# Moving the gating of w_down into the up-projection's stage, and one level of the recurrence's copies to ScalarE

## The chip, the core and the metric

The kernel runs on one core of one Trainium2 chip. The metric is the device time of one launch in microseconds; before the change it is 2444.8 us (median of three runs, 2444.23 to 2445.5). Five engines work in parallel, each in its own order: TensorE (PE) multiplies matrices, VectorE (DVE), ScalarE (ACT) and GpSimd (POOL) work elementwise, and SyncE (SP) issues nearly all DMA transfers. An instruction that has to wait holds up everything behind it on its engine; on SP that is every later transfer.

## The reference

One layer of a hybrid backbone on 2048 latent tokens of width 1024 (and 256 context tokens), in float32:

```
h  = modulate(rmsnorm(x), sh1, sc1)
o  = token_mixers(h @ w_in)        # HGRN2 recurrence (4 heads) and gMLP spatial gating (4 heads)
x  = x + g1 * (o @ w_out)
h2 = modulate(rmsnorm(x), sh2, sc2)
x  = x + g2 * ((a * gelu(conv3x3(g))) @ w_down)     # a, g = split(h2 @ w_up), 2816 columns each
out = rmsnorm(x)
```

The gates g1 and g2 are vectors over the 1024 output columns, computed from c and w_ada. Since g2 multiplies every row of the last product alike, the kernel multiplies the columns of w_down by g2 once and stores the result ("gating of w_down"). The recurrence is evaluated in chunks of 128 positions by doubling: within a chunk the scores between positions are filled in by levels of 1, 2, 4, ... 64, where a level B holds the pairs in neighbouring blocks of B positions.

## The kernel before, in words

The kernel runs in four stages after a short start (first 100 us: modulation vectors and the context).

1. Input projection and recurrence, to about 980 us. `run_banks` walks over column blocks of w_in: 24 matmuls of 128x512 per bank, in three terms (high and low parts of both operands, float32r). Between them `slot()` asks two queues whether the next piece of other work is due: `hg_q` holds the recurrence of the previous head (`hg`), `bg_q` the background work. Due times are kept in `T.t`, a clock that adds up the expected time of every issued matmul; a generator yields how many us of it must pass before its next piece. In order, the background holds eight blocks of the modulation (`ada_block`), the gating and splitting of w_out (`w_out_ops`), the convolution's taps (`conv_taps`), and the gating of w_down (`w_down_ops`).
2. Output projection and second norm, to about 1169 us. Its results, prepared as seven operands of a Strassen-like product, partly stay in SBUF and partly go through DRAM (`yd`); the staging tiles have the tag `yst`, two buffers.
3. Up-projection and convolution, to about 2014 us: 308 products of 12 matmuls each, two units (a `g` unit and an `a` unit, two column blocks of w_up each) interleaved in groups of 14. Each product's weights are loaded as `raw` halves (512 KB), split by `prep` three products ahead (`LOOK = 3`): ScalarE casts the high part `Ah`, GpSimd subtracts to get the low part `Al`, four buffers each. The 12 matmuls take the high part first, eight times, then the low part four times. `after` empties the PSUM banks (`ux`, `uz`, two each): copies `keep` on ScalarE, additions on VectorE. The convolution is nine taps over a 128x1024 tile: one on ScalarE (L1431), eight on VectorE (L1434, in place in PSUM tile `dn`), then GELU on ScalarE. Results go to DRAM as `m`, edge rows through `gs` and `as`.
4. Down-projection, to the end: seven products of 11 column pairs, operands `m` and the gated w_down (`wd_d`, eleven DRAM tiles) read back and split. It reads the gated w_down first shortly before the third stage ends.

`T.t` decides where work is written into the program. After that a planner orders the instructions of each engine by its own expected times; `pin(...)` keeps an instruction in the order in which it was written. Neither knows the time that the chip takes.

The gating of w_down (L997 to L1011) takes two halves of the columns: g2 broadcast to 128 partitions (L1004), and for each of 11 row pairs a load of 512 KB into a `raw` tile (L1007; three buffers, shared with the loads of w_in, L221), a pinned VectorE multiplication of 128x1024 (L1009) and a store (L1010).

In a recurrence level, TensorE forms the products of a level for eight chunks in two banks of tag `sc`. Levels up to 32 are merged into the score tile `sc` with a predicated VectorE copy by a mask (L846, 128x512), the level of 64 by two ScalarE copies of 64 partitions x 4 x 64 (L843, L844). After each level VectorE scales Q (`level_update`, L513), K is scaled and copied (`level_keys`, VectorE or GpSimd L590, ScalarE L593), and the totals are multiplied (`next_tot`, L520).

Of the kernel before, what the change touches and what calls it, by code (L numbers as in the profile page):

```python
# [9 lines left out]
F32 = mybir.dt.float32  # L10
F32R = mybir.dt.float32r
# [7 lines left out]
P = 128  # L19
# [9 lines left out]
NF = FF // P  # L29
# [4 lines left out]
AL = 512  # L34
# [14 lines left out]
def view(t, off, dims):  # L49

    return bass.AP(t.tensor, t.offset + off, [list(t.ap[0])] + [list(d) for d in dims])
# [32 lines left out]
def tile_trunk(ctx, tc, x, c, cx, c_ctx, w_ada, b_ada, norm_mix, norm_ffn, w_in, hg_norm, sgu_g, sgu_b,  # L84
               w_sp, b_sp, w_out, w_up, conv_w, conv_b, w_down, norm_final, masks, out):
    nc = tc.nc
    V, S, G, T = nc.vector, nc.scalar, nc.gpsimd, Tensor(nc.tensor)
    ld = nc.sync.dma_start
    st = nc.sync.dma_start
    pin = tc.keep_in_program_order  # L90

    x = x[0]
    w_ada, w_in, w_out, w_up, w_down = w_ada[0], w_in[0], w_out[0], w_up[0], w_down[0]
# [21 lines left out]
    g_d = dr.tile([2, D], F32, name="g_d")  # L115
# [4 lines left out]
    wd_d = [dr.tile([P, 2, D], F32, name=f"wd{j}") for j in range(NF // 2)]  # L120
# [62 lines left out]
    hg_q, bg_q = Pump(), Pump()  # L183
# [7 lines left out]
    with es1:  # L191
        ps = es1.enter_context(tc.tile_pool(name="ps1", bufs=1, space=PSUM, reuse_waits="tile"))
        p1 = es1.enter_context(tc.tile_pool(name="p1", bufs=1, reuse_waits="tile"))
        pm = es1.enter_context(tc.tile_pool(name="pm", bufs=1, reuse_waits="tile"))
# [19 lines left out]
        def raw_tile():  # L214
            return p1.tile([P, D], F32, tag="raw", name="raw", bufs=3)
# [51 lines left out]
        acc = ph.tile([P, 2, 512], F32, tag="qs", name="acc")  # L267
# [523 lines left out]
        def hg(hh, h, F, K, qs, vt, sgt):  # L791
# [33 lines left out]
            for l, B in enumerate(LV):  # L825
                dims = [[2 * B, P // (2 * B)], [TH + B, 2], [1, B]]
                if B < 4:
                    dims = [[TH + B, 2], [2 * B, P // (2 * B)], [1, B]]
                if B == P // 2:
                    dims = dims[1:]  # L830
                for g in range(0, NCH, 4):
                    pb = bank("sc")
                    if B == 1:
                        column_sums(pb, knh[g // 4], knl[:, g * P:g * P + 512])
                    for i in range(4) if B > 1 else ():
                        off = (g + i) * P
                        o = pb[:, i * P:(i + 1) * P]
                        if B < 4:
                            o = view(pb, i * P, [[B, 2], [2 * B, P // (2 * B)], [1, B]])
                        T.matmul(o, K[:, 0, off:off + P], view(Q, off, dims), start=True, stop=True)  # L840
                    if B == P // 2:
                        pq = pb.rearrange("p (c t) -> p c t", t=P)
                        S.copy(sc[:B, g:g + 4, B:], pq[:B, :, B:])  # L843
                        S.copy(sc[B:, g:g + 4, :B], pq[B:, :, :B])  # L844
                        continue
                    V.copy_predicated(sc[:, g:g + 4, :], view(msk, l * P, [[0, 4], [1, P]]),  # L846
                                      pb.rearrange("p (c t) -> p c t", t=P))
                level_update(Q, TH, B, tot, False)
                K, K2 = level_keys(K, B, tot, K2), None
                tot = next_tot(tot, TH, B)  # L850
                yield 4.2
# [144 lines left out]
                    st(wo_d[:, k, 1, cl], g)  # L996
                    yield 2.5  # L997

        def w_down_ops():

            for n in range(2):
                cl = slice(n * 512, n * 512 + 512)
                g = pm.tile([P, 512], F32, tag="acc", name="g2")
                ld(g, g_d[1:2, cl].broadcast_to([P, 512]))  # L1004
                for j in range(NF // 2):
                    raw = raw_tile().rearrange("p (a c) -> p a c", a=2)
                    ld(raw, w_down[2 * j * P:2 * (j + 1) * P, cl].rearrange("(a p) c -> p a c", p=P))  # L1007
                    yield 9.0
                    pin(V.tensor_mul(raw, raw, view(g, 0, [[0, 2], [1, 512]])))  # L1009
                    st(wd_d[j][:, :, cl], raw)  # L1010
                    yield 2.5  # L1011

        def silu(dst, scale):
            def f(n0, n, pj):
                t = pm.tile([P, 512], F32, tag="sig", name="sig", bufs=2)
# [4 lines left out]
        def head(hh, h):  # L1020
# [18 lines left out]
            def pre_g():  # L1039
                if prev[0] >= 0:  # L1040
                    need(hg_q, (prev[0], prev[1], "keys"))
                else:
                    need(bg_q, "x1")
                    for e in range(8):
                        bg_q.add(ada_block(e))
                    bg_q.add(w_out_ops())
                    bg_q.add(conv_taps())
                    bg_q.add(w_down_ops())
                t["F"] = pk.tile([P, 2, TH], F32, tag="F", name="F", align_bytes=AL)
                t["K"] = pk.tile([P, 2, TH], F32, tag="K", name="K", bufs=2, align_bytes=AL)  # L1050

# [479 lines left out]

    NJ = NF // 2

    def a_src(r, c, j):
        return m_d[2 * j + c][:, r * TH:(r + 1) * TH]

# [30 lines left out]
    for n, (u, i) in enumerate(prods):  # L1567
# [20 lines left out]
        if n == 12:  # L1588
            edges = px.tile([P, 7, P], F32R, tag="yst", name="edges", bufs=2, align_bytes=AL).bitcast(F32)
            edges = edges[:, :4, :].rearrange("p f (w c) -> p f w c", w=2)  # L1590
        with tc.issue_after(scaled[-1].ins) if n < 8 else nullcontext():
            after(u, i, p)
        for j in range(7):
# [13 lines left out]
            cast(j, early[j], wr[j], (mhl[:, j, 0, :], mhl[:, j, 1, :]),  # L1607
                 [t.rearrange("p a b -> p (a b)") for t in a_tiles()])
        conv_step() and conv_step()
    assert not work  # L1610
    while stores:
        stores.pop(0)[1]()
    esp.close()
# [250 lines left out]
```

## Time and profile before

| what | us |
|---|---|
| median of three runs | 2444.8 |
| profiled execution | 2441.35 |
| its span, first to last instruction | 2439.6 |
| TensorE busy | 2403.6 (99%) |
| VectorE busy | 1669.5 (68%) |
| ScalarE busy | 1039.4 (43%) |
| GpSimd busy | 882.7 (36%) |

The profile is one execution; times in its rows are us from the span's start, and durations marked "mean" or min/median/max are ns. The page gives busy time by engine; other views group instructions by line and tile, give busy time by stretches, list who waited for whom (in total, times, longest), and show a stretch in order of time. In the timeline a row is: start, length, engine, line, operation, output tile and inputs, form, count, and in brackets the idle time before it and what ended it. "SPq" is SP's queue of transfers; its rows show when a transfer is issued, not when it lands. Consecutive rows of a kind are merged, and matmuls overlap, so a matmul shows 0.39 us while the next starts 0.227 us after it. Line numbers are those of the kernel before.

### The profile page before, as it was taken

The numbers are of one execution on the slowest core, as the hardware profiler recorded it, in microseconds if no ns is written. First come the engines' busy times: TensorE is split into PE (matmuls) and PEld (weight loads), VectorE is DVE, ScalarE is ACT, GpSimd is POOL, SyncE is SP. The second block draws the span as 40 slices with busy tenths as digits, with TensorE's granted clock in tenths as the row PEclk, the third lists the DMA queues.
The fourth block names the chain that finished last, engine by engine and source line by source line (L and its number), as shares of the span: only waits on it lengthen the run. The fifth ranks groups of instructions, "written<-read, shape, count | busy, mean of one in ns | idle before, by whom it ended". The sixth has DMA issues, their size and how long they took to land.

```text
span 2439.6 us, 32382 instructions
## 1 busy us (share of the span) xinstructions
PE 2403.6 (99%) x11711; PEld 1995.0 (82%) x11711; DVE 1669.5 (68%) x2293; ACT 1039.4 (43%) x1802; POOL 882.7 (36%) x796
## 2 busy tenths in 40 slices
PE   8999999999999999999999999999999999999998
PEld 5887887888888887788888888888888887888887
DVE  5867795756776786465596666639866772776875
ACT  4554334434444443354554444434445442332343
POOL 1232110110121132000688778787888870000002
PEclk9999999999999999999999999999999999999999
DMA  8365446573354323768922322562222238934745
GB/s 311 108 209 163 152 136 196 193 241 121 113 177 156 104 104 141 239 209 260 309 82 86 97 81 91 183 230 97 86 94 86 88 112 334 324 121 147 229 153 196
DMA packets 307853, 400.10 MB, mean 164 GB/s; under 512 B 33113, under 2 KB 216161, under 8 KB 304621
## 3 DMA queue, kind: packets, MB, share of 16 engines
q1 hardware_dynamic: 304404, 397.28, 48.3%
q8 instruction: 92, 1.51, 0.2%
q10 hardware_dynamic: 3289, 0.76, 0.1%
q14 instruction: 68, 0.56, 0.1%
HBM read 288.85 MB, written 109.13 MB: 163 GB/s over the span
## 4 chain that ended last, share of the span: by engine, by line
PE 47%; issue 2%; POOL 1%; DVE 1%; ACT 1%; SPq 0%; DMA 0%; POOLq 0%; ACTq 0%
PE ux L65 19%; PE uz L65 14%; PE dn L65 14%; POOL ra L1723 0%; POOL rr L1724 0%; DVE dn L1434 0%; POOL Al L134 0%; ACT mhl L133 0%; ACT jk L1715 0%; DVE odd L80 0%; ACT odd L1793 0%; DVE mhl L80 0%; DVE thl L80 0%; ACT thl L133 0%; POOL raw L1243 0%
## 5 line engine op out<-in xcount | busy, mean ns | idle before, releaser
L1434 DVE SCALAR_TENSOR_TENSOR dn<-gp,taps,dn 128x1024 f32<-128x1024 f32 x352 | 448.3, 1285 | 97.2 <-ACT dn L1431 92.8
L65 PE MATMUL dn<-thl,mhl 128*128 128x512 f32 x1680 | 381.5, 389 | 1.2 <-ACT thl L133 1.2
L65 PEld LDWEIGHTS dn<-thl,mhl 128*128 128x128 f32 x1680 | 315.1, 188 | 67.6 <-ACT thl L133 2.1
L134 POOL TENSOR_TENSOR Al<-raw,Ah 128x512 fp32r<-128x512 f32 x264 | 341.3, 1309 | 69.3 <-ACT Ah L133 40.5
L65 PE MATMUL pj<-xh,whi 128*128 128x512 f32 x896 | 362.4, 405 | 0.0
L65 PE MATMUL pj<-xl,whi 128*128 128x512 f32 x896 | 351.3, 392 | 0.6 <-POOL xl L134 0.6
L65 PE MATMUL pj<-xh,wlo 128*128 128x512 f32 x896 | 350.9, 392 | 0.9 <-DVE wlo L134 0.9
L133 ACT CAST Ah<-raw 128x512 fp32r<-128x512 f32 x264 | 163.0, 620 | 240.4 <-PE ux L65 134.6
L65 PE MATMUL ux<-xah,Ah 128*128 128x512 f32 x528 | 205.7, 390 | 0.3 <-ACT keep L1498 0.3
L65 PEld LDWEIGHTS pj<-xh,wlo 128*128 128x128 f32 x896 | 168.4, 188 | 36.9 <-DVE wlo L134 1.1
L65 PEld LDWEIGHTS pj<-xh,whi 128*128 128x128 f32 x896 | 168.9, 189 | 33.7 <-issue 3.5
L65 PEld LDWEIGHTS pj<-xl,whi 128*128 128x128 f32 x896 | 169.1, 189 | 31.9 <-POOL xl L134 1.5
L65 PE MATMUL dn<-wo,o 128*128 128x512 f32 x768 | 182.9, 394 | 1.7 <-DVE nt L717 0.9
L65 PE MATMUL uz<-yf,Ah 128*128 128x512 f32 x704 | 174.0, 389 | 0.0
L590 POOL TENSOR_TENSOR K<-K,tot 128x512 f32<-128x512 f32 x40 | 58.3, 1458 | 303.8 <-DVE tot L520 158.0
L65 PEld LDWEIGHTS dn<-wo,o 128*128 128x128 f32 x768 | 142.0, 188 | 31.6 <-issue 1.1
L65 PE MATMUL ux<-yf,Ah 128*128 128x512 f32 x528 | 155.4, 389 | 0.0
L65 PEld LDWEIGHTS uz<-yf,Ah 128*128 128x128 f32 x704 | 132.1, 188 | 27.4
L65 PE MATMUL ux<-xah,Al 128*128 128x512 f32 x528 | 141.7, 390 | 1.0 <-POOL Al L134 1.0
L65 PE MATMUL ux<-xal,Ah 128*128 128x512 f32 x352 | 137.1, 389 | 0.0
L1723 POOL TENSOR_SCALAR ra<-ss 128x1 f32<-128x1 f32 x8 | 5.3, 662 | 360.4 <-ACT jk L1715 360.4
L134 DVE TENSOR_TENSOR wlo<-raw,whi 128x1024 fp32r<-128x1024 f32 x68 | 85.1, 1252 | 72.6 <-ACT whi L133 70.7
(345 smaller groups left out, 4480.5 us busy)
## 6 DMA issues: line engine op xcount, KB each, us to landing
raw<-in_w_up_dram SPq DMA_DIRECT2D x88, 512.0 KB
mr<-m SPq DMA_DIRECT2D x85, 512.0 KB
raw<-in_w_in_dram SPq DMA_DIRECT2D x68, 512.0 KB
sT<-wd SPq DMA_DIRECT2D x88, 256.0 KB
raw<-in_w_ada_dram SPq DMA_DIRECT2D x32, 512.0 KB
yf<-yd SPq DMA_DIRECT2D x14, 1024.0 KB
m<-cv SPq DMA_DIRECT2D x22, 544.0 KB
raw<-in_w_down_dram SPq DMA_DIRECT2D x22, 512.0 KB
```

The source lines that it names most:

```text
L65: return self.engine.matmul(out, lhsT, rhs, **kw)
L133: keep(S.copy(hi, raw))
L134: (eng or G).tensor_sub(lo, raw, hi.bitcast(F32))
L590: e.tensor_mul(view(K2, row * W + o, src), view(K, o, src), view(tot, t0, [[4, n], [ts, 2], [0, B]]))
L1434: V.scalar_tensor_tensor(out=cr, in0=gt[:, t // 3:t // 3 + RH, t % 3:t % 3 + GW], scalar=taps[:, t * NF + f:t * NF + f + 1], in1=cr, op0=A ...
L1723: G.tensor_scalar(out=a, in0=ss, scalar1=plus, scalar2=None, op0=ALU.add)
```

## The change

Two edits.

The level of 32 of the recurrence is merged as the level of 64 is: its blocks are copied by ScalarE, four blocks of 32 partitions x 4 chunks x 32 columns for each of the two banks. The predicated VectorE copy remains for the levels of 1 to 16.

The gating of w_down leaves the background of the first stage. In the third stage a new generator with the same name is added to `bg_q` at the product n = 12. It takes four quarters of 256 columns instead of two halves of 512, so that there are 44 items: a load of 256 KB, a multiplication of 128x512 on VectorE, a store of 256 KB; and four broadcast loads of g2. All use a single tile: one of the two `yst` buffers (the tile `edges` has the other). The multiplication is no longer pinned. The loop over products asked `bg_q.slot()` at every third matmul already.

```diff
-                    if B == P // 2:
+                    if B > 16:
                         pq = pb.rearrange("p (c t) -> p c t", t=P)
-                        S.copy(sc[:B, g:g + 4, B:], pq[:B, :, B:])
-                        S.copy(sc[B:, g:g + 4, :B], pq[B:, :, :B])
+                        for r in range(0, P, B):
+                            o = r ^ B
+                            S.copy(sc[r:r + B, g:g + 4, o:o + B], pq[r:r + B, :, o:o + B])
                         continue
...
-        def w_down_ops():
-
-            for n in range(2):
-                cl = slice(n * 512, n * 512 + 512)
-                g = pm.tile([P, 512], F32, tag="acc", name="g2")
-                ld(g, g_d[1:2, cl].broadcast_to([P, 512]))
-                for j in range(NF // 2):
-                    raw = raw_tile().rearrange("p (a c) -> p a c", a=2)
-                    ld(raw, w_down[2 * j * P:2 * (j + 1) * P, cl].rearrange("(a p) c -> p a c", p=P))
-                    yield 9.0
-                    pin(V.tensor_mul(raw, raw, view(g, 0, [[0, 2], [1, 512]])))
-                    st(wd_d[j][:, :, cl], raw)
-                    yield 2.5
...
-                    bg_q.add(w_down_ops())
...
+    def w_down_ops():
+
+        t = px.tile([P, 7, P], F32R, tag="yst", name="wd", bufs=2, align_bytes=AL).bitcast(F32)
+        t = t.rearrange("p a b -> p (a b)")
+        g, raw = t[:, :256], t[:, 256:768].rearrange("p (a c) -> p a c", a=2)
+        for n in range(4):
+            cl = slice(n * 256, n * 256 + 256)
+            ld(g, g_d[1:2, cl].broadcast_to([P, 256]))
+            for j in range(NJ):
+                ld(raw, w_down[2 * j * P:2 * (j + 1) * P, cl].rearrange("(a p) c -> p a c", p=P))
+                yield 5.0
+                V.tensor_mul(raw, raw, view(g, 0, [[0, 2], [1, 256]]))
+                yield 2.5
+                st(wd_d[j][:, :, cl], raw)
+                yield 4.5
...
         if n == 12:
             edges = px.tile([P, 7, P], F32R, tag="yst", name="edges", bufs=2, align_bytes=AL).bitcast(F32)
             edges = edges[:, :4, :].rearrange("p f (w c) -> p f w c", w=2)
+            bg_q.add(w_down_ops())
```

More of the change, by code (lines that the diff above doesn't have):

```diff
@@ L1609, in tile_trunk @@
         conv_step() and conv_step()
-    assert not work
+    assert not work and not bg_q.tasks
     while stores:
```

## The prediction

> **What bounds the kernel now.** I read the page first, then the busy times by stage, then the waits of TensorE by stage, then the timelines of one steady stretch of the up-projection. From the page and the stages (columns: stretch, its length, busy us and instructions of each engine, granted clock, DMA share, GB/s):
>
> ```profile
> span 2439.6 us, 32382 instructions
> PE 2403.6 (99%) x11711; PEld 1995.0 (82%) x11711; DVE 1669.5 (68%) x2293; ACT 1039.4 (43%) x1802; POOL 882.7 (36%) x796
> 549.00:834.00 285.00, 282.69 (x1592) 243.47 (x1592) 206.65 (x292) 122.26 (x250) 44.60 (x39) 1.00 0.42 140
> 834.00:980.00 146.00, 139.80 (x823) 120.01 (x822) 97.70 (x200) 55.83 (x143) 36.51 (x39) 1.00 0.34 121
> 1210.00:1250.00 40.00, 39.02 (x172) 31.65 (x171) 37.13 (x37) 20.06 (x33) 32.77 (x29) 1.00 0.35 104
> 1250.00:1560.00 310.00, 310.00 (x1369) 256.71 (x1368) 216.76 (x206) 135.99 (x220) 251.44 (x215) 1.00 0.28 89
> ```
>
> TensorE is the bound, with 36 us of idle time in the whole span. The gating of w_down now lies at 545 to 832 us; there TensorE idles 285.00 - 282.69 = 2.3 us. The stage it moves to has no idle time at all after 1250, but GpSimd is at 251.44/310 = 81% and VectorE at 70%. So the removal can give back little, and the question is whether the new place stays hidden. What TensorE waits for, first at 525 to 834, then (last two rows) at 1169 to 2014:
>
> ```profile
> PE sc L65 <- DVE Q L513: 0.7, 2, 0.5
> PE mi L69 <- DVE nt L709: 0.7, 1, 0.7
> PE sc L65 <- DVE knl L822: 0.6, 1, 0.6
> PE mi L69 <- ACT kt L861: 0.2, 1, 0.2
> PE ux L65 <- POOL Al L134: 1.0, 2, 0.7
> PE ux L65 <- ACT keep L1498: 0.3, 1, 0.3
> ```
>
> **Part 1: out of the recurrence's stage.** Gone are 22 multiplications, 22 loads, 22 stores and 2 broadcast loads:
>
> ```profile
> L1009 DVE TENSOR_TENSOR raw<-raw,g x22: 1209/1217/2314, 544.8 to 831.9; 128x1024 f32<-128x1024 f32 x22
> 715.69 1.21 DVE L1009 TENSOR_TENSOR raw<-raw,g 128x1024 f32<-128x1024 f32 x1
> ```
>
> That is 22 x 1.217 = 26.8 us of VectorE, beside a TensorE that hardly waits. Two of its waits end a dense VectorE run that holds a gating multiplication: the one for knl (0.6, at 706 us) and one of the two for Q (at 719 us, behind the row at 715.69). I put them at -0.8 us together. The ends: -2.3 (all idle time of that stretch goes) and 0. SP's queue loses 46 issues and the waits that go with them, but no wait of TensorE there names a w_in load, so that is nothing. In the built order TensorE's own sequence differs in two places only, both where score products of the last level move a few matmuls ahead.
>
> **Part 2: the level of 32.** Per head and half, two predicated copies (VectorE) become eight ScalarE copies of 32 partitions x 128 elements:
>
> ```profile
> L846 DVE COPY_PREDICATED sc<-msk,sc x96: 709/734/772, 232.1 to 921.7; 128x512 f32<-128x512 uint8 x96
> L809 ACT COPY sc<-sc x16: 579/590/604, 224.9 to 879.2; 128x512 f32<-128x512 f32 x16
> L843 ACT COPY sc<-sc x16: 366/366/367, 269.7 to 926.5; 64x256 f32<-64x256 f32 x16
> ```
>
> VectorE loses 16 x 0.734 = 11.7 us. From 512 to 256 elements a copy falls by 0.22 us, so 128 elements are about 0.25 us (an estimate from the two ScalarE rows): 64 x 0.25 = 16 us more on ScalarE, which is at 43% in this stretch (122.26/285). For one head the next level's scaling starts 1.5 us sooner and the score bank comes free 8 x 0.25 - 1.5 = 0.5 us later. I take 0: the next product of that kind comes 4.2 us of issued matmuls later. The ends: +4 us (0.5 us on TensorE's path in all eight passes) and -3 us (half of the 6.2 us of idle time at 834 to 980, where VectorE is named most).
>
> **Part 3: into the up-projection.** 44 items of load (256 KB), multiplication 128x512, store, and 4 broadcast loads, all through one buffer: each load waits on SP for the store before it to land. The waits written in the code add to 12 us, but the multiplication is not pinned, and the planner places five items in each 14 products (14 x 12 matmuls at 0.227 us = 38.1 us). SP's built order there is: w_up, w_up, store, load, gs, store, w_up, load, w_up, as, gs, store, load, m, as, m, store, load, store, load. I lay it over a steady stretch:
>
> ```profile
> 1384.25 0.38 SPq L1218 DMA_DIRECT2D raw<-in_w_up_dram  x1
> 1387.98 1.29 POOL L1237 TENSOR_TENSOR raw<-raw 128x512 f32<-128x512 f32 x1 [2.51 <-DMA raw<-in_w_up_dram]
> L993 DVE TENSOR_TENSOR raw<-raw x16: 664/692/694, 373.6 to 500.6; 128x512 f32<-128x512 f32 x16
> SPq L1007 <- DMA wd<-raw: 25.1, 11, 3.3
> 1402.42 5.26 DVE L1434 SCALAR_TENSOR_TENSOR dn<-gp,taps,dn 128x1024 f32<-128x1024 f32 x4
> 1406.98 0.32 SPq L1481 DMA_DIRECT2D m<-cv  x1
> 1410.05 0.69 DVE L1508 TENSOR_TENSOR gp<-uz,keep 128x512 f32<-128x512 f32 x1 [2.37 <-PE uz L65]
> 1415.95 0.38 SPq L1218 DMA_DIRECT2D raw<-in_w_up_dram  x1
> 1420.66 0.84 PE L65 MATMUL uz<-yf,Ah 128*128 128x512 f32 x3
> ```
>
> 512 KB are there 3.7 us after the issue starts (1384.25 to 1387.98); I take 2.9 for 256 KB, and 2.3 for a store (25.1/11, what SP waited for one of twice the size). A multiplication is 0.69 us. The tightest piece: the store behind m at 1407.3 lands at 1409.7, the next load at 1412.6, its multiplication ends at 1413.3 (1413.9 if GpSimd holds it up), that store lands at 1416.2, one more load is issued by 1416.6, and only then the w_up load that now starts at 1415.95: some 0.7 to 1.2 us late. VectorE's order puts that multiplication ahead of the addition at 1410.05, which ends near 1414.6 instead of 1410.7; TensorE writes that bank again at 1420.66 only. The slip does not add up from one stretch to the next, since SP waits for m's product again each time. What hides it must be priced too:
>
> ```profile
> 1408.16 1.28 POOL L1239 TENSOR_TENSOR fl<-raw 128x512 f32<-128x512 f32 x1
> 1409.48 0.62 ACT L133 CAST Ah<-fl 128x512 fp32r<-128x512 f32 x1 [4.35 <-POOL fl L1239]
> 1412.03 1.28 POOL L134 TENSOR_TENSOR Al<-fl,Ah 128x512 fp32r<-128x512 f32 x1
> 1414.43 0.58 ACT L1498 COPY keep<-ux 128x512 f32<-128x512 f32 x1
> 1417.03 1.07 PE L65 MATMUL ux<-xah,Al 128*128 128x512 f32 x4
> 1417.94 0.39 PE L65 MATMUL ux<-xah,Ah 128*128 128x512 f32 x1
> 1213.04 1.89 POOL L134 TENSOR_TENSOR Al<-raw,Ah 128x512 fp32r<-128x512 f32 x1 [2.29 <-ACT Ah L133]
> 1212.69 1.08 DVE L134 TENSOR_TENSOR fl<-fl,yst 128x896 fp32r<-128x896 f32 x1
> ```
>
> The smallest margins of a stretch are 1417.03 - 1413.31 = 3.7 us (low part of a weight) and 1417.94 - 1415.01 = 2.9 us (copy that empties a bank). Against them stands GpSimd's loss: it took 1.89 instead of 1.28 us where a VectorE subtraction with both inputs in SBUF ran beside it. The new multiplication has both inputs in SBUF as well, so I charge GpSimd about 0.6 us an item, 5 x 0.6 = 3 us in 38, where it now idles 7. At most two items fall into the dense run ahead of these margins: 1.2 us of 2.9. So 0 for the steady part; the ends are 0 and +16 us (2 us in each of eight stretches).
>
> The Trainium skill ("SBUF — State Buffer", Who interferes with whom) says that such a VectorE instruction and a GpSimd instruction that reads SBUF exclude each other for a whole instruction. The trace agrees (0.6 us above). By that rule GpSimd would lose 44 x 0.69 = 30 us over some 340, 81% to 90% busy, which alone changes no term.
>
> The entry has no such margin. TensorE already waits for the low part twice:
>
> ```profile
> 1220.11 1.20 PE L65 MATMUL ux<-xah,Al 128*128 128x512 f32 x4 [0.33 <-POOL Al L134]
> 1226.49 1.20 PE L65 MATMUL ux<-xah,Al 128*128 128x512 f32 x4 [0.65 <-POOL Al L134]
> 1226.53 7.24 DVE L1434 SCALAR_TENSOR_TENSOR dn<-gp,taps,dn 128x1024 f32<-128x1024 f32 x6
> 1228.99 6.67 SPq L1218 DMA_DIRECT2D raw<-in_w_up_dram  x2
> 1244.13 0.69 DVE L1515 TENSOR_TENSOR cv<-ux,cv 128x512 f32<-128x512 f32 x1
> 1252.02 0.39 PE L65 MATMUL ux<-xah,Ah 128*128 128x512 f32 x1
> ```
>
> The first item is multiplied near 1219.7, between taps; GpSimd runs without a gap there, so its 0.6 us goes straight to the wait at 1226.49: +0.65 us. The second load stands on SP behind the w_up load at 1228.99, lands near 1232.6, and VectorE waits for it since about 1228: some 5 to 6 us late through its dense run. The product that empties a bank at 1244.13 may slip 1252.02 - 1244.82 = 7.2 us. So it just holds. Value +0.65; ends 0 and +6 (later loads, and the GELU behind the late taps holding ScalarE).
>
> **Sum**, against the profiled execution (span 2439.6, 2441.35 us in all): -0.8 + 0 + 0 + 0.65 = -0.15. The median of the runs is 3.45 us above that execution, so 2444.8 - 0.15 = 2444.6.
>
> **Rivals.** (1) Slower, the steady part: SP's chain of store, load, multiplication is longer than I take it. It decides when the chain is 2.9 - 1.2 = 1.7 us longer per stretch than my 2.3 and 2.9 make it; beyond that every us costs eight. At 3 us more: 8 x 1.3 = 10 us, 2455. For it: SP's longest wait for a store was 3.3, 1 us over my value; against: that store was twice the size. (2) Slower, the entry alone: VectorE over 7.2 us late there and GpSimd late as well, 5 to 6 us, 2450. For it: no margin at 1226; against: it happens once. (3) Faster: VectorE's backlog, not those two waits, makes the idle time of the recurrence's stage; all 2.3 us go, and the 3 us of part 2: 2444.8 - 5.3 = 2439.5. Against it: most of the idle time at 834 to 980 lies past the last gating. (4) The change doesn't spread the work: planner and buffer push several items together. The built order shows five in 38 us, so this falls under (1).
>
> **How the numbers follow.** No measurable change 0.60; (1) 0.20; (2) 0.09, both past 0.2% (4.9 us, about what a measurement of this kernel can tell from no change); (3) 0.11. So faster 0.11, same 0.60, slower 0.29. The range reaches from (3) to just past (1): 2439 to 2457. The likeliest case's own range is 2441 to 2449.
>
> **What would show it.** Right: no gating in the recurrence's stage and its idle time down by about 1 us; TensorE at 310 of 310 us from 1250; waits for the low part near 1226 a little longer; GpSimd's instructions beside the new multiplications near 1.9 us; w_up issues at most 2 us later per stretch. Wrong: waits of TensorE for the low part or the keep copy that return every 38 us, or VectorE waiting long for the w_down load in each stretch.

## The result and the profile after: 2487.0 us, slower by 1.7%

The changed kernel takes 2487.0 us (median of five runs, 2483.86 to 2488.83); the kernel before takes 2445.18 us beside it (median of five). The ratio is 1.017, with a 95% interval of 1.0155 to 1.0185. The forecast was 2444.6 us, with a range of 2439 to 2457.

The page of the changed kernel: span, busy times, and the first line of the chain that ended last. Line numbers in the rows of the changed kernel are its own: the load of w_down is L1529, its multiplication L1531, its store L1533, the load of w_up L1204, the copy `keep` L1484 on ScalarE, the additions that empty PSUM banks L1494, L1501 and L1503 on VectorE, the taps L1420.

```profile
span 2487.0 us, 32518 instructions
PE 2419.7 (97%) x11711; PEld 1998.8 (80%) x11711; DVE 1679.5 (68%) x2299; ACT 1051.3 (42%) x1866; POOL 897.3 (36%) x796
PE 36%; DMA 8%; issue 3%; POOL 3%; DVE 2%; ACT 1%; SPq 1%; POOLq 0%; ACTq 0%; DVEq 0%
```

The span grew by 2487.0 - 2439.6 = 47.4 us. TensorE ran the same 11711 matmuls. It was idle for 2487.0 - 2419.7 = 67.3 us in place of 36.0, which is 31.3 us more, and it was busy for 16.1 us longer with the same work. So there are two parts: waiting, and a longer busy time, of which some 10 us are matmuls that ran slower (below). DMA now stands in the chain with 8%; the same line of the page of before reads:

```profile
PE 47%; issue 2%; POOL 1%; DVE 1%; ACT 1%; SPq 0%; DMA 0%; POOLq 0%; ACTq 0%
```

The busy time by stretches shows where (columns as in the forecast: stretch, length, busy us and instructions of PE, weight loads, DVE, ACT and POOL, granted clock, DMA share, GB/s):

```profile
549.00:834.00 285.00, 283.46 (x1602) 244.97 (x1601) 182.91 (x265) 130.81 (x282) 40.77 (x39) 1.00 0.19 63
834.00:980.00 146.00, 140.48 (x827) 120.78 (x826) 94.73 (x196) 57.37 (x151) 34.74 (x39) 1.00 0.35 122
1210.00:1250.00 40.00, 38.64 (x170) 31.31 (x169) 34.40 (x35) 18.13 (x30) 32.26 (x28) 1.00 0.50 146
1250.00:1560.00 310.00, 289.48 (x1216) 231.01 (x1215) 228.25 (x222) 118.30 (x196) 235.14 (x191) 0.97 0.44 139
```

The recurrence's stage became a little better: its idle time at 549 to 834 us fell from 2.3 to 1.5 us. The up-projection became much worse: TensorE idles 20.5 of 310 us, where it idled 0, it gets through 1216 matmuls instead of 1369, and the mean granted clock is 0.97. What TensorE waits for from 996 to 2030 us (total, times, longest), and then, for VectorE and for SP's queue, the largest waits on w_down's items:

```profile
PE ux L65 <- DVE cv L1501: 13.9, 5, 3.4
PE ux L65 <- POOL Al L134: 6.2, 10, 1.0
PE uz L65 <- DVE gp L1494: 6.1, 1, 6.1
PE ux L65 <- ACT keep L1484: 2.1, 6, 1.0
```

```profile
DVE wd L1531 <- DMA wd<-in_w_down_dram: 101.2, 27, 7.5
SPq L1529 <- DMA wd<-wd: 86.3, 39, 4.0
SPq L1533 <- DVE wd L1531: 74.5, 25, 4.8
```

VectorE stands in front of 27 of the 44 multiplications for 101.2 us in total, until the load of w_down has landed. SP stands for 86.3 us until a store has landed (the next load goes into the same buffer), and for 74.5 us until a multiplication is done. TensorE's largest wait, for `cv` of L1501, is for a VectorE addition that stands behind such a multiplication.

One turn of the chain in order of time, in the changed kernel: SP's issues, then VectorE, then TensorE (start, length, instruction, in brackets the idle time before it and what ended it).

```profile
1444.84 0.37 SPq L1204 DMA_DIRECT2D raw<-in_w_up_dram  x1
1445.26 0.53 SPq L1533 DMA_DIRECT2D wd<-wd  x1
1449.78 0.38 SPq L1529 DMA_DIRECT2D wd<-in_w_down_dram  x1
...
1453.59 0.53 SPq L1533 DMA_DIRECT2D wd<-wd  x1
1454.21 0.56 SPq L1204 DMA_DIRECT2D raw<-in_w_up_dram  x1
1456.37 0.37 SPq L1529 DMA_DIRECT2D wd<-in_w_down_dram  x1
1456.83 0.42 SPq L1204 DMA_DIRECT2D raw<-in_w_up_dram  x1
```

```profile
1452.53 1.03 DVE L1531 TENSOR_TENSOR wd<-wd 128x512 f32<-128x512 f32 x1 [4.43 <-DMA wd<-in_w_down_dram]
1453.49 0.68 DVE L1503 TENSOR_TENSOR keep<-uz,keep 128x512 f32<-128x512 f32 x1
1461.06 1.12 DVE L1531 TENSOR_TENSOR wd<-wd 128x512 f32<-128x512 f32 x1 [6.89 <-DMA wd<-in_w_down_dram]
1462.10 1.28 DVE L1420 SCALAR_TENSOR_TENSOR dn<-gp,taps,dn 128x1024 f32<-128x1024 f32 x1
1463.29 0.68 DVE L1501 TENSOR_TENSOR cv<-ux,cv 128x512 f32<-128x512 f32 x1
```

```profile
1460.13 1.07 PE L65 MATMUL ux<-xah,Al 128*128 128x512 f32 x4
1464.11 0.77 PE L65 MATMUL ux<-xah,Ah 128*128 128x512 f32 x1 [2.92 <-DVE cv L1501]
1465.10 0.63 PE L65 MATMUL ux<-xah,Ah 128*128 128x512 f32 x1
```

The store issued at 1445.26 right behind a 512 KB load of w_up holds the next load until 1449.78, 4.5 us. That load is used at 1452.53, 2.75 us later. The next store holds its load from 1453.59 to 1456.37, 2.8 us. The load behind it is issued 2.2 us behind one w_up load and just ahead of another, and is used at 1461.06, 4.7 us later. VectorE does nothing for 6.89 us, although taps and the addition of L1501 stand behind the multiplication. The addition comes at 1463.29, and TensorE, which wanted to write that bank at 1461.2, has waited 2.92 us. Then its matmuls take 0.63 us instead of 0.39. TensorE's longest waits come at the same place of each group of 14 products: at products 71, 85, 99, 113 and 127 for `cv`, and at 141 for `gp`.

The slower matmuls are the granted clock. Four stretches of half clock, each of which begins in the last 0.3 to 1.7 us of such a wait, by the same columns as above:

```profile
1374.60:1378.00 3.40, 3.14 (x8) 2.49 (x9) 3.37 (x5) 0.08 (x1) 0.68 (x1) 0.51 0.41 139
1463.40:1470.20 6.80, 6.09 (x14) 4.79 (x15) 6.76 (x8) 0.59 (x1) 2.07 (x3) 0.50 0.43 154
1552.10:1558.90 6.80, 5.68 (x13) 4.47 (x14) 6.76 (x8) 1.72 (x3) 3.37 (x5) 0.50 0.46 159
1599.90:1606.70 6.80, 5.10 (x12) 4.07 (x13) 6.76 (x8) 1.21 (x2) 4.83 (x5) 0.50 0.53 194
```

Together these are 23.8 us at half speed. TensorE was busy in 20.0 us of them (3.14 + 6.09 + 5.68 + 5.10) and still waited in the rest, so the half speed costs about 20.0 / 2 = 10 us. The kernel before has no such stretch in the up-projection.

How the delay grows, worked out from the two traces: the start of the first matmul of product n in the changed kernel, less the same start before, less the difference at n = 0 (2.4 us, which belongs to what lies ahead of this stage; the nine runs below with the same edits there enter it between 1.6 us earlier and 0.3 us later than before, so it is not shown to come from the edits).

| product n | 28 | 56 | 84 | 98 | 112 | 126 | 140 | 154 | 307 |
|---|---|---|---|---|---|---|---|---|---|
| us later | 0.3 | 1.0 | 9.8 | 16.2 | 22.8 | 28.7 | 36.3 | 45.0 | 45.0 |

From about product 70 each group of 14 products adds 6 to 9 us, until the items run out near product 147. Nothing is won back afterwards.

### The profile page after: what moved, and what is told of

Same layout as the page of the kernel before. It is cut to its first block, busy times and chain, and to the rows that moved or that the text cites. A ratio compares the mean times of both kernels' runs of the same rounds, so it can differ in the third digit from the quotient of the medians.

```text
span 2487.0 us, 32518 instructions
## 1 busy us (share of the span) xinstructions
PE 2419.7 (97%) x11711; PEld 1998.8 (80%) x11711; DVE 1679.5 (68%) x2299; ACT 1051.3 (42%) x1866; POOL 897.3 (36%) x796
## 4 chain that ended last, share of the span: by engine, by line
PE 36%; DMA 8%; issue 3%; POOL 3%; DVE 2%; ACT 1%; SPq 1%; POOLq 0%; ACTq 0%; DVEq 0%
PE dn L65 13%; PE ux L65 13%; PE uz L65 10%; DMA wd<-wd 3%; DMA wd<-in_w_down_dram 2%; DMA raw<-in_w_up_dram 2%; POOL Al L134 1%; DMA as<-cv 1%; DVE wd L1531 1%; DVE dn L1420 0%; POOL cv L1504 0%; POOL ra L1726 0%; DMA sT<-wd 0%; POOL rr L1727 0%; POOL fl L1225 0%
## 5 line engine op out<-in xcount | busy, mean ns | idle before, releaser
L1420 DVE SCALAR_TENSOR_TENSOR dn<-gp,taps,dn 128x1024 f32<-128x1024 f32 x352 | 447.4, 1283 | 44.3 <-ACT dn L1417 40.7
L134 POOL TENSOR_TENSOR Al<-raw,Ah 128x512 fp32r<-128x512 f32 x264 | 351.5, 1348 | 60.5 <-ACT Ah L133 38.9
L65 PE MATMUL ux<-xah,Ah 128*128 128x512 f32 x528 | 210.1, 398 | 16.2 <-DVE cv L1501 13.9
```

Source lines behind the costliest of these rows:

```text
L65: return self.engine.matmul(out, lhsT, rhs, **kw)
L134: (eng or G).tensor_sub(lo, raw, hi.bitcast(F32))
L1420: V.scalar_tensor_tensor(out=cr, in0=gt[:, t // 3:t // 3 + RH, t % 3:t % 3 + GW], scalar=taps[:, t * NF + f:t * NF + f + 1], in1=cr, op0=A ...
```

## The experiments

Theory A, formed from this profile: an item is a chain (store, load, multiplication, store) through one buffer, the program's order puts its links closer together than the transfers allow, and VectorE and SP, which work in order, pass the lateness on to work that TensorE needs. Rivals: (B) the level of 32 on ScalarE has its part in it; (C) the multiplications themselves, or their exclusion of GpSimd, are the cost; (D) SP alone is the link, since w_up's loads stand behind w_down's; (E) the traffic is the cost, in whatever order. "Loss" below is the median less the median of the kernel before on the same chip. "Pace" is products per item times the 2.72 us of a product (12 matmuls at 0.227), counted from the products beside which the first and the last load are issued: 43 steps over products 17 to 143 in the changed kernel, so 2.9 products or 8 us.

| run | what | loss, us | ratio | 95% interval |
|---|---|---|---|---|
| e1 | the move alone | +44.9 | 1.0187 | 1.0173 to 1.0201 |
| e2 | level of 32 alone | -1.0 | 0.9995 | 0.9986 to 1.0004 |
| e3 | multiplication pinned, pace 12.6 us | +11.9 | 1.0046 | 1.0033 to 1.0059 |
| e4 | multiplications alone | +2.2 | 1.001 | 1.0001 to 1.0019 |
| e5 | transfers alone, pace 5.6 us | +12.6 | 1.0052 | 1.0032 to 1.0072 |
| e6 | multiplication pinned, pace 8 us | +16.5 | 1.007 | 1.0055 to 1.0085 |
| e7 | three buffers of half size, pace 8 us | +9.4 | 1.004 | 1.0028 to 1.0053 |
| e8 | e3 with a pause | +3.4 | 1.0016 | 1.0006 to 1.0025 |
| e9 | e7 on ScalarE's queue | +20.0 | 1.0082 | 1.0067 to 1.0097 |
| e10 | load pinned, multiplication free, pace 12.8 us | +17.8 | 1.0079 | 1.0065 to 1.0093 |
| e11 | transfers alone, pace 8 us | +5.4 | 1.0023 | 1.0013 to 1.0033 |
| e12 | e8, one item in some 15 us | -2.7 | 0.9989 | 0.9981 to 0.9998 |

### The move alone and the level of 32 alone

e1 is the changed kernel with the level of 32 as before; e2 is the kernel before with only that level changed.

```diff
# e1, against the changed kernel
-                    if B > 16:
-                        for r in range(0, P, B):
-                            o = r ^ B
-                            S.copy(sc[r:r + B, g:g + 4, o:o + B], pq[r:r + B, :, o:o + B])
+                    if B == P // 2:
+                        S.copy(sc[:B, g:g + 4, B:], pq[:B, :, B:])
+                        S.copy(sc[B:, g:g + 4, :B], pq[B:, :, :B])
# e2, against the kernel before: the same lines the other way round
```

> Only the gating is moved; the level of 32 is merged by the predicated copy as before. Chain theory (the items' load, multiplication and store through one buffer, in SP's and VectorE's fixed orders, make VectorE wait and TensorE after it, about 45 us between 1290 and 1620): 2482 to 2488, the long waits of VectorE for the w_down load as in the changed kernel. Level theory (the ScalarE copies delay the recurrence): 2465 or less. Port theory (VectorE and GpSimd block each other): 2482 to 2488 too.

> Only the level of 32 goes to ScalarE; the gating stays in the first stage. Chain theory: 2443 to 2448, so no change; the 2.4 us by which the changed kernel enters the up-projection late appear here only if they come from the copies. Level theory: 2455 or more.

e1 loses 44.9 us, as much as both edits together (41.8); e2 loses nothing (-1.0 us, interval -3.4 to +1.0). In e2 the steady stretch of the up-projection is untouched:

```profile
1250.00:1560.00 310.00, 310.00 (x1370) 256.70 (x1369) 216.74 (x206) 137.21 (x223) 251.66 (x215) 1.00 0.28 89
```

Rival B falls. The loss comes from moving w_down's items.

### The multiplication pinned

```diff
-                V.tensor_mul(raw, raw, view(g, 0, [[0, 2], [1, 256]]))
+                pin(V.tensor_mul(raw, raw, view(g, 0, [[0, 2], [1, 256]])))
```

> The changed kernel with the multiplication pinned to the written order, as it was before the change; the planner then places about three items in 38 us instead of five. Chain theory: the chain of some 9 us per item no longer fills the time, 2444 to 2452, waits of VectorE for the load under 20 us in all. Port theory: as many multiplications beside GpSimd as before, 2475 or more. Level theory: no change against the changed kernel, 2480 or more.

One word in the code takes 30 us of the changed kernel's 41.8 away. At 2455.2 us it stays above the 2444 to 2452 expected. It changes two things at once: the multiplications stand where the code writes them, and the pace falls from one item in 8 us to one in 12.6, because the planner no longer draws the items together. VectorE's waits for the load fall to about a third, though not under the 20 us expected:

```profile
DVE wd L1531 <- DMA wd<-in_w_down_dram: 36.8, 13, 5.7
PE ux L65 <- POOL Al L134: 7.5, 6, 4.5
```

The delay, worked out as above, reads 5.1 us by product 168 and then 13.2 by product 182, in one step of 8.2 us. There a wait of TensorE for a low part stands in the timeline, and 6.8 us of half clock from 1662.6, which is before that wait ends:

```profile
1657.68 2.11 PE L65 MATMUL ux<-yf,Ah 128*128 128x512 f32 x8 [0.68 <-ACT keep L1484]
1664.28 2.07 PE L65 MATMUL ux<-yf,Al 128*128 128x512 f32 x4 [4.48 <-POOL Al L134]
```

### The multiplications alone

```diff
+    def mul_ops():
+        t = px.tile([P, 7, P], F32R, tag="yst", name="wd", bufs=2, align_bytes=AL).bitcast(F32)
+        t = t.rearrange("p a b -> p (a b)")
+        g, raw = t[:, :256], t[:, 256:768].rearrange("p (a c) -> p a c", a=2)
+        V.memset(t[:, :768], 1.0)
+        for n in range(44):
+            yield 7.0
+            pin(V.tensor_mul(raw, raw, view(g, 0, [[0, 2], [1, 256]])))
...
+            bg_q.add(mul_ops())
```

> The kernel before, with 44 further multiplications of 128x512 on a tile of ones in the up-projection, pinned, one each 7 us of issued matmuls, and no transfer with them; the gating stays in the first stage. This is the work of the change on VectorE and beside GpSimd, without the chain. Chain theory: 2445 to 2448. Port theory: 2470 or more.

44 multiplications of the same shape cost 2.2 us (interval 0.2 to 4.6), though each of them takes 1.13 us in the mean:

```profile
L1542 DVE TENSOR_TENSOR wd<-wd 128x512 f32<-128x512 f32 x44 | 49.8, 1132 | 0.0
```

Rival C falls as the main cause.

### The transfers alone

In e5 the multiplications are left out; loads, stores and waits stay.

```diff
                 yield 5.0
-                V.tensor_mul(raw, raw, view(g, 0, [[0, 2], [1, 256]]))
                 yield 2.5
```

> The changed kernel without the 44 multiplications: w_down is loaded and stored again ungated, so this part of the computation is left out. SP's chain (each load waits for the store before it to land, each store for its load) stays, VectorE takes no part in it. If TensorE loses its time through VectorE, which waits for the loads with the taps and bank additions behind it: 2445 to 2455, and no waits of TensorE for VectorE. If it loses it through SP, where the w_up loads stand behind the chain: 2470 or more, with waits for the low parts.

It loses 12.6 us, between its two cases. But this is not the share of SP and of the traffic in the whole loss: without a multiplication the planner draws the items still closer together, to 2.07 products (5.6 us) an item, so this was not the changed kernel's pace. e11 repeats it with the load pinned and shorter waits in the code, which brings the items back to 8 us:

```diff
-                ld(raw, w_down[2 * j * P:2 * (j + 1) * P, cl].rearrange("(a p) c -> p a c", p=P))
-                yield 5.0
-                yield 2.5
+                pin(ld(raw, w_down[2 * j * P:2 * (j + 1) * P, cl].rearrange("(a p) c -> p a c", p=P)))
+                yield 3.3
+                yield 1.9
                 st(wd_d[j][:, :, cl], raw)
-                yield 4.5
+                yield 2.6
```

> The run without multiplications again (w_down is stored ungated, so the gating is what this kernel leaves out), but with its items at the changed kernel's pace, one in some 8 us, where the run without multiplications had one in 5.9 us. It measures what the loads and stores alone cost at that pace. If the transfers and their waits on SP make the 15 to 20 us that are left when VectorE's order is written out, it takes 2453 to 2460 us; if that loss needs the multiplications, it falls to 2449 us or less.

2449.5 us, a loss of 5.4 (interval 3.2 to 8.1): between the two cases, nearer to the one in which most of the loss needs the multiplications. Its waits of TensorE are short ones:

```profile
PE ux L65 <- POOL Al L134: 4.6, 9, 1.0
PE ux L65 <- ACT keep L1484: 3.1, 8, 1.0
```

So the traffic and SP's order (D and E) cost some 5 us at this pace, and more the denser the items stand.

### The written order at the changed kernel's pace

e6 is e3 with waits of 3.3, 1.9 and 2.6 us in place of 5.0, 2.5 and 4.5: pinned multiplications, and again one item in 8 us.

```diff
-                yield 5.0
+                yield 3.3
                 pin(V.tensor_mul(raw, raw, view(g, 0, [[0, 2], [1, 256]])))
-                yield 2.5
+                yield 1.9
                 st(wd_d[j][:, :, cl], raw)
-                yield 4.5
+                yield 2.6
```

> As the pinned kernel, with the waits in the code shortened from 12 to 7.8 us (8.2 by the steps of the clock), so that about five items fall into 38 us as in the changed kernel, but in the written order. If the pace of a single buffer is the cause: 2475 to 2495. If the planner's own placing of the multiplication is: 2460 or less.

At 2461.5 us it loses 16.5, far nearer to the case of the planner's own placing (2460 or less) than to that of the pace. VectorE still waits for loads, but less, and it holds up TensorE four times instead of six:

```profile
DVE wd L1531 <- DMA wd<-in_w_down_dram: 69.1, 26, 8.3
PE uz L65 <- DVE gp L1494: 8.4, 4, 3.6
```

At one and the same pace, then: transfers alone 5.4, with multiplications in the written order 16.5, with multiplications where the planner puts them 41.8 (the changed kernel itself). In e6's profiled execution 6.1 us of the delay arise at the entry of the stage, by product 28, at one wait of 3.56 us for `gp` of L1494 with 3.4 us of half clock; the changed kernel has 0.3 us there.

### The planner's multiplications at the slow pace

e10 pins the load and leaves the multiplication free, which holds the pace at 12.8 us and gives the planner back its choice on VectorE.

```diff
-                ld(raw, w_down[2 * j * P:2 * (j + 1) * P, cl].rearrange("(a p) c -> p a c", p=P))
+                pin(ld(raw, w_down[2 * j * P:2 * (j + 1) * P, cl].rearrange("(a p) c -> p a c", p=P)))
```

> The changed kernel with w_down's loads pinned in the order of SP, as the code's waits write them (one item in some 12.6 us), and the multiplications left to the planner as in the changed kernel (one item in some 8 us there). It tells the pace of the items from the place that the planner gives the multiplications on VectorE. If the place is the larger cause, VectorE still stands 3 to 7 us ahead of many of them and the time is 2465 to 2485 us. If the pace is, the items have time to land whatever the order, and the time is that of the run with pinned multiplications, 2450 to 2458 us.

2462.0 us, between the two expectations, so neither the place nor the pace explains the loss alone. VectorE stands in front of the multiplications almost as long as in the changed kernel, but with more time between the items it passes less of it on:

```profile
DVE wd L1531 <- DMA wd<-in_w_down_dram: 86.6, 28, 7.8
PE ux L65 <- POOL Al L134: 11.4, 8, 6.2
```

The four runs form a square (loss in us): written order 11.9 at 12.6 us and 16.5 at 8 us, planner's order 17.8 at 12.8 us and 41.8 at 8 us. The two causes strengthen each other. In e10's profiled run 12.4 us of the delay again arise in one step between products 168 and 182: a wait of 2.2 us for `keep` ends at 1663.8, 13.7 us of half clock begin at 1665.1, and the wait of 6.2 us lies inside them.

### Three buffers, and another queue

e7 breaks the chain through the single buffer: 88 items of 128 columns, three buffers, the load issued one item ahead. e9 is e7 with loads and stores issued on ScalarE's queue.

```diff
# e7, against e3
+        raws = [t[:, P + 256 * i:P + 256 * i + 256].rearrange("p (a c) -> p a c", a=2) for i in range(3)]
+        items = [(n, j) for n in range(8) for j in range(NJ)]
...
+        fetch(0)
+        for k, (n, j) in enumerate(items):
+            if k + 1 < len(items):
+                fetch(k + 1)
+            yield 2.0
+            raw = raws[k % 3]
+            pin(V.tensor_mul(raw, raw, view(g, 0, [[0, 2], [1, P]])))
...
+            yield 1.7
+            st(wd_d[j][:, :, n * P:n * P + P], raw)
# e9, against e7
-            ld(raws[k % 3], w_down[2 * j * P:2 * (j + 1) * P, n * P:n * P + P].rearrange("(a p) c -> p a c", p=P))
+            S.dma_start(raws[k % 3], w_down[2 * j * P:2 * (j + 1) * P, n * P:n * P + P].rearrange("(a p) c -> p a c", p=P))
...
-            st(wd_d[j][:, :, n * P:n * P + P], raw)
+            S.dma_start(wd_d[j][:, :, n * P:n * P + P], raw)
```

> The same bytes at the same pace, pinned, in 88 items of half the size (128 columns) through three buffers, each load issued one item ahead: a load no longer waits for the store just before it, and a multiplication not for its own load. If the single buffer's waits are the cause: 2444 to 2456. If the traffic and the number of transfers on SP are: 2475 or more.

> The kernel of the run with three buffers of half size, with w_down's loads and stores issued on ScalarE's queue in place of SP's; SP then issues w_up's loads without standing behind a wait for w_down's store, load or multiplication. If SP's order is the link between the chain and TensorE, the waits for GpSimd's low part go and the time is 2450 us or less. If the traffic itself is the cost (the same bytes in the same time), it stays at 2453 us or more. If ScalarE, which now stands behind the waits for the store and the multiplication, takes the place of SP, the waits of TensorE for the keep copy grow and the time is above 2455 us.

e7 loses 9.4 us, 7 less than e6 with the same bytes at the same pace. The longer time from load to multiplication helps, and some loss stays; its longest wait of TensorE is for `keep` (3.7 us), at the entry again, where 6.2 us of the delay in its profiled execution arise. e9 loses 20.0 us, the third case of its expectation: ScalarE now stands in front of issues that wait for a store or a multiplication, and the copy that TensorE waits for stands behind them.

```profile
PE ux L65 <- ACT keep L1484: 10.1, 10, 1.6
PE ux L65 <- POOL Al L134: 7.4, 9, 1.1
```

The low part needs ScalarE's cast first, so this row, too, is ScalarE's lateness or that of the traffic; which of the two wasn't separated. The Trainium skill ("DMA: Bandwidth & Descriptors", Issuing engines are not separate DMA queues) says that transfers issued by different engines run on the same 16 DMA engines, and that spreading them saves issue time only. This run agrees in that the other queue gained nothing (20.0 against 9.4 us lost).

### The meeting with the larger loads, and a slow pace

e8 is e3 with the items suspended from product 138 to 172, where the 1 MB loads of `yf` stand in SP's queue; e12 also stretches the waits to 6.0, 3.0 and 5.4 us.

```diff
# e8, against e3
             for j in range(NJ):
+                while 138 <= now[0] <= 172:
+                    yield 2.0
# e12, against e8
-                yield 5.0
+                yield 6.0
...
-                yield 2.5
+                yield 3.0
...
-                yield 4.5
+                yield 5.4
```

> The kernel of the pinned run, in which w_down's items are suspended while the up-projection is between products 138 and 172, the stretch in which the 1 MB loads of the trunk's output stand in the same queue. In the pinned run the delay rose there by 8.2 us in one step, after a wait of TensorE for GpSimd's low part. If that step comes from the meeting of the items with these loads, it goes, and the time is 2446 to 2450 us (the 5.0 us that the pinned run had lost by product 126 stay). If the step is the items' own pace, which would then be met before or after the pause, the time stays at 2453 us or more.

> The run with the pause, at a slower pace: one item in some 15 us, so that they fill the up-projection to its last products. If the loss goes with the pace, the 3.4 us that the run with the pause had lost fall to between 0 and 2 us: 2444 to 2446 us beside a kernel before of 2444. If a loss of 3 us or more stays, it comes from the items themselves and not from their pace. Faster than before by at most the 0.8 us that the recurrence's stage gave back.

With the pause the step of 8.2 us is gone and the loss is 3.4 us: that step came from the items in this stretch. That the 1 MB loads make it is likely and not shown alone: in e3 the store issued at 1595.9 right behind one of them took 12.5 us to land and the load at 1608.5 took 8.2, but TensorE's long wait begins some 40 us behind the issue of the last of them, and the pause also takes away items that stand closer to it. In the trace of e8 3.7 us of the delay arise instead between products 200 and 220, behind the pause. At the slower pace the rest goes as well. The delay through the whole up-projection is 0.9 us in the trace, TensorE has hardly a wait from 996 to 2030 us, and the steady stretch is full:

```profile
PE ux L65 <- POOL Al L134: 2.1, 2, 1.1
PE ux L69 <- DVE cv L1265: 1.3, 3, 1.0
```

So the items as such cost nothing; 44 loads, multiplications and stores fit into this stage if they stand far enough apart and away from the large loads. e12 takes 2441.5 us beside 2444.2 (ratio 0.9989, 0.9981 to 0.9998): 2.7 us faster in the median, where its expectation allowed 0.8 at most. The interval ends just below 1, and the difference is about 0.1%, so this is no gain to build on. It is the best version found.

## Why the prediction was wrong

**Part 1, the recurrence's stage: right.** -0.8 us was forecast; the idle time at 549 to 834 us fell from 2.3 to 1.54 us, and it is 1.5 us in e1, e3, e8, e10 and e12, too (2.7 in e2, where the gating stays).

**Part 2, the level of 32: right.** 0 was forecast; e2 gave -1.0 us (-3.4 to +1.0). The estimate of 0.25 us a copy stands beside 0.258 us in this row of the changed kernel (min, median, max over both forms; the shorter one has 64 of the 96 copies, so the median is one of them):

```profile
L845 ACT COPY sc<-sc x96: 238/258/370, 264.7 to 925.5; 32x128 f32<-32x128 f32 x64, 64x256 f32<-64x256 f32 x32
```

**Part 3, the entry: right, at about half the size.** +0.65 us was forecast with "So it just holds"; the idle time at 1210 to 1250 us rose from 0.98 to 1.36 us, the delay is 0.3 us by product 28, and the bank behind VectorE's dense run didn't become the wait.

**Part 3, the steady part: this is the step that failed.** It found the order of SP as it was then built, five items in 14 products. Then it priced one piece of that order as the tightest, the one behind m (store, load, store, load, w_up), and put the steady part at 0. That piece came out as priced:

```profile
1427.73 0.53 SPq L1533 DMA_DIRECT2D wd<-wd  x1
1430.55 0.39 SPq L1529 DMA_DIRECT2D wd<-in_w_down_dram  x1
1434.17 0.53 SPq L1533 DMA_DIRECT2D wd<-wd  x1
1436.56 0.39 SPq L1529 DMA_DIRECT2D wd<-in_w_down_dram  x1
1437.04 0.44 SPq L1204 DMA_DIRECT2D raw<-in_w_up_dram  x1
```

From the store behind m to the w_up load it is 9.3 us here, and 9.3 to 9.7 us in the five turns from 1383 to 1562 us; the forecast had 9.3 (1407.3 to 1416.6). The piece that fails is the one after it, at the head of the order (w_up, store, load, gs, store, w_up, load), which the forecast didn't price. It is the turn shown above: from the store at 1445.26 to the end of the second multiplication at 1462.18 the terms were 4.5 + 2.75 + 1.03 + 2.8 + 4.7 + 1.12 = 16.9 us, where the forecast's prices give 2.3 + 2.9 + 0.69 + 2.3 + 2.9 + 0.69 = 11.8. In the six turns from 1355 us on it took 15.6 to 17.2 us, up to the next store.

The reason is that it took one duration for each kind of transfer: "I take 2.9 for 256 KB, and 2.3 for a store". Over all 44 items, from the start of the issue to the landing as the forecast counts, the medians are 2.75 us for a load and 2.74 for a store. So the load was priced well as a typical one, and the store 0.4 us too low: the 25.1/11 it rests on is the time that SP still had to wait, while the 512 KB stores of before took 3.1 us in the median from issue to landing. But the two transfers issued within 2.2 us behind a 512 KB load took 1.6 and 2 times their price, the other two about what was taken. The multiplication was mis-sized too, 1.04 us in the median against 0.69:

```profile
L1531 DVE TENSOR_TENSOR wd<-wd x44: 685/1041/1762, 1222.4 to 1610.6; 128x512 f32<-128x512 f32 x44
```

From these 5 us follows the second error, "The slip does not add up from one stretch to the next, since SP waits for m's product again each time". It does add up, by 6 to 9 us each 14 products. The lateness doesn't reach TensorE through SP alone: VectorE stands before the multiplication, behind it stand the additions that empty the PSUM banks, and when TensorE waits for such a bank, everything behind moves with it, m's product too, so that the next stretch starts from the same tight place. The forecast let one such addition slip by 4 us and checked the bank of that one product; it didn't ask what happens to L1501 behind the second multiplication. In the kernel before, that addition (L1515 there) ends at 1397.42 and its bank is written again at 1404.34, 6.9 us later. The 5 us, the tap that now stands between multiplication and addition (1.2 us) and the second w_up load coming 7.8 in place of 6.4 us behind the first make 7.7, which by this rough sum uses that up.

The third was left out altogether: during and after such waits the granted clock is half for 3.4 or 6.8 us, about 10 of the 45 us.

**The rivals.** Rival (1), the chain of store, load and multiplication longer than taken, is what happened, though in another piece of the order and by way of VectorE's addition. Its threshold of 1.7 us was passed by 5.1 - 1.7 = 3.4 us, and by the forecast's eight stretches that is 27 us; with the 10 us of half clock it makes 37 of the 42 to 45 lost. As the threshold was worked out for the piece behind m, this tells the size only, and that it comes so near is partly luck. (The trace has six stretches in which the loss arises, products 70 to 154, with 7.0 us each in the mean, half clock included.) Its price of 10 us assumed 3 us in excess, where 5 were measured, and its chance of 0.20 rested on the one longest wait for a store of before (3.3 us). Rival (4), that the planner pushes items together, was counted under (1); e3, e6 and e10 show that the closeness has its own price. Rivals (2) and (3) didn't come in the changed kernel; something like (2), a loss of 6 us at the entry, did in e6 and e7. GpSimd's exclusion, charged at nothing, was rightly so: single subtractions rose from at most 1.33 to 1.83 us, as the next rows show, first of before and then of after (GpSimd from 1220 to 1600 us), but e4 with 44 multiplications loses only 2.2 us.

```profile
L134 POOL TENSOR_TENSOR Al<-raw,Ah x121: 1282/1296/1328, 1220.0 to 1597.2; 128x512 fp32r<-128x512 f32 x121
```

```profile
L134 POOL TENSOR_TENSOR Al<-raw,Ah x108: 1258/1297/1832, 1222.3 to 1598.9; 128x512 fp32r<-128x512 f32 x108
```

**What would show it wrong** was named: "VectorE waiting long for the w_down load in each stretch", and that is the largest row of VectorE's waits after.

What stays open: the split of e6's 16.5 us between the entry, the tail of the transfer times and SP's order (e7 gets 7 of it back with two changes at once, buffers and look-ahead); whether the 1 MB loads alone make the late step of e3; and why the planner draws free multiplications together.

## What to carry to other kernels

Before moving background work into a stage with a full engine, write its chain of transfers through one buffer as a sum for every piece of the order, not only for the one that looks tightest, with the durations that transfers have behind the stage's own large loads, not their typical ones, and compare that with the time that the program's order leaves. An in-order engine that meets an instruction whose load hasn't landed stops everything behind it, so put the instruction where the load is surely there (pin it, spread the items, keep them away from the largest loads): the same 44 items cost 42 us in one order and pace and nothing in another. When the engine that bounds the kernel is made to wait for some 2 us or more, count the slower clock that can follow as well.

## What the runs showed of the hardware

The granted clock halves when TensorE idles for about 2 us within one window of 3.4 us, and the windows lie on a fixed grid. In the changed kernel the stretches of half clock shown above begin 88.8, 88.7 and 47.8 us apart, which is 26, 26 and 14 times 3.41 us, and they last 3.4 or 6.8 us (13.7 in e10). With the grid laid out from these beginnings, the idle time of TensorE (by the busy times of the profile) was summed in each window that starts at full clock, in all 14 traces from 140 us to 60 us before the end. With 1.95 us of idle time or more the next window was at half clock in 26 of 26 cases, with 1.78 to 1.92 us in 5 of 7, with 1.67 us or less in none, among them 90 cases of 0.9 us or more. So the length of a wait alone doesn't decide: the wait of 2.92 us that ends at 1464.11 has 2.2 us in the window before 1463.4 and is followed by half clock, while one of 2.86 us that ends at 1508.70 is split by the border at 1507.8 into 1.9 and 0.9 us and is not; in e6 a wait of 2.30 us was enough. The Trainium skill ("TensorE: Matmul & The Clock Gate", the part on the clock gate) says that the clock is half after at least one idle window of about 3.4 us, in windows that run freely. The lengths and the grid agree; here a window needn't be idle throughout.

A 256 KB load or store takes 2.7 to 2.8 us from the start of the issue to the landing in the median, but the slowest tenth takes 4.5 to 5.3 us as a load and 4.3 to 4.5 as a store (all 44 of each in the changed kernel); in the timeline above the slow ones are those issued close behind 512 KB loads.

A VectorE multiplication with both inputs in SBUF takes 0.69 us at the least, 1.04 us in the median in the up-projection beside GpSimd, and up to 1.76 us; GpSimd's subtraction takes 1.30 us in the median and up to 1.83. The Trainium skill ("SBUF — State Buffer", Who interferes with whom) describes an exclusive lock between such an instruction and a GpSimd instruction that reads SBUF. The numbers of both engines agree.
